# Feed-forward's first product by seven products of quarters instead of eight, and the mixing's streams in another order

## The chip, the cores and the metric

One core of a Trainium2 chip runs the whole program in one launch. The metric is device time in microseconds. Before the change three runs took 2124.88, 2127.32 and 2127.90 us (median 2127.32).

## The reference

The program is a decoder trunk of two layers over 512 tokens and 16 learned meta tokens (528 columns), model width 1024. Each layer is a half-step SwiGLU feed-forward, a token mixing of four head groups, and a second feed-forward; each has an RMS norm before and behind it. What matters here is the feed-forward:

```python
h = h + 0.5 * rms_norm(swiglu(rms_norm(h, g[0]), ffn_w_in[l, 0], ffn_w_out[l, 0]), g[1])

def swiglu(x, w_in, w_out):                 # w_in 1024 x 5120, w_out 2560 x 1024
    gate, up = jnp.split(x @ w_in, 2, axis=-1)
    return (jax.nn.silu(gate) * up) @ w_out
```

The mixing is one input product of 2476 columns, forgetting attention, a 31-tap convolution module, a gated linear recurrence, a sparse attention with a top-128 selection by an indexer, and an output product.

## The kernel before

Activations lie transposed: 128 features per tile, tokens as columns, in two halves of 264 columns (`half`, L433). The last feed-forward drops the meta tokens and has halves of 256 columns. Each fp32 operand of a large product is written as a sum of two fp32r parts, hi and lo; a product of one 128 x 128 weight tile with one tile of x is three matmuls (hi·hi, hi·lo, lo·hi; `product`, L536). A weight tile is brought by SyncE's DMA queue into one of two `raw` buffers, ScalarE copies it to hi, and VectorE (in places GpSimd) subtracts to get lo (`weight`, `wsplit`, L502 to L531). Six pairs of hi and lo buffers rotate: three of the pool `weights` and three in spare rings (`SPARE`).

The feed-forward (`ffn`, L833) goes over 20 blocks j of 128 hidden features, in chunks of 6, 6 and 8. For each block it needs a gate and an up product, each over 8 tiles of the model width, for each token half. x holds `h*g` without the norm's row factor R; `gated` (L772) multiplies both sums by R as it reads them from PSUM (VectorE), applies Silu (ScalarE), multiplies the two (GpSimd), and splits the result into G hi (ScalarE) and G lo (VectorE). In the last feed-forward the two halves are one product of 512 columns. Blocks 0 to 2 of each feed-forward (`lead`) are interleaved with the norm ahead of it. When a chunk's blocks are done, the output product adds its part to `y` (chunks 0 and 1 in `ffn`, the last one in `tail`, or in `ffn_out_tokens` for the last feed-forward).

The PSUM banks are tagged u, a and n, with 2, 5 and 1 of them (`BANKS = 251`); `pu` (L482) rotates over the seven of u and a. Temporaries of one half come from the tag `t1`, five buffers.

Two things set the order of instructions. In `ffn` it is the framework's scheduler, which takes the first instruction in program order that is ready in its own timeline. In start, mixing and the passages between feed-forwards it is `Weave` (L108 to L375): each piece of work is a stream with a rank (`RANK`), the planner has a cost for every instruction (`cost`, L199) and takes the earliest start, the lower rank among near ones; the order on each engine is then kept. `ENG` and `SUMS` say which elementwise work goes to VectorE (V), GpSimd (G) or to whichever the planner finds better (E). `ND` is the number of the 30 convolution taps per channel block that VectorE does; GpSimd and ScalarE do the others.

Of the kernel before, what the change touches and what calls it, by code (L numbers as in the profile page):

```python
# [16 lines left out]
P = 128  # L17
# [33 lines left out]
def shape_constants():  # L51
# [6 lines left out]
    c[:, C_MASK : C_MASK + 530] = np.where(j - p <= 424, 0.0, NEG)  # L58
# [49 lines left out]
class Weave:  # L108
# [13 lines left out]
    AHEAD = dict(PE=0.0, A=0.05, V=0.0, G=0.3)  # L122
# [59 lines left out]
    def ported(self, key, op, aps, reads):  # L182

        if key == "G":
            return True
        if key != "V" or any(a.space == bass.MemoryType.PSUM for a in aps) or op in ("max", "match_replace"):
            return False
        return True

    def free(self, key, ported, t):  # L190

        if not ported or key not in "VG":
            return t
        for begin, end in self.port["G" if key == "V" else "V"]:
            if begin <= t < end:
                t = end
        return t

    def cost(self, key, op, aps, args, reads, start):  # L199
# [3 lines left out]
        if key == "PE":  # L203
            if op == "transpose":
                n = args[1].shape[0]
                return self.pace(start, 0.091, n * n / 128 / 2400)
            cols, rows = args[2].free_size(), args[2].shape[0]
            if cols == 1:
                return 0.156
            if args[2].dtype == F32R:  # L210
                return self.pace(start, max(cols / 2400 + 0.0115, 0.092), cols * rows / 128 / 2400)
            return self.pace(start, max(cols * 4 / 2400 + 0.005, 0.184), cols * rows / 128 / 1200)
# [9 lines left out]
    def issue(self, key, op, call, args, kw):  # L222
# [9 lines left out]
        if key == "E":  # L232
            ways = {
                k: (self.ready(k, chip, writes), self.cost(k, op, aps, args, reads, 0.0), self.ported(k, op, aps, reads))
                for k in "VG"
            }
            if s:
                self.park(s, ("E", ways))
            key = self.either(ways)
            call, ready, _, ported = call[key], *ways[key]  # L240
        else:
            ready = self.ready(key, chip, writes)
            ported = self.ported(key, op, aps, reads)
            if s and key != "Q":
                self.park(s, (key, ready, ported))
# [3 lines left out]
        start = self.free(key, ported, max(ready, self.clock[key]))  # L249
# [5 lines left out]
        if ported:  # L255
            self.port[key] = sorted(self.port[key][-11:] + [(start, end)])
# [85 lines left out]
    def start_of(self, s):  # L342
# [7 lines left out]
        ready, ported = (what + [True])[:2]  # L350
        if kind == "E":
            kind = self.either(ready)
            ready, _, ported = ready[kind]
        return self.free(kind, ported, max(ready, self.clock[kind])), kind
# [22 lines left out]
class Trunk:  # L377
# [17 lines left out]
    KEPT = ("PE", "A", "V", "G")  # L395
    RANK = dict(ev=0, late=48.5, weights=18.0, row=179.1, lead=42.0, index=212.2, prep=19.1, scores=52.9,
                dsa=144.3, topk=187, fox=42.6, lru=14.4, lrub=76.1, first=92.5, turn0=1.5, turn1=25,
                start0=136.2, start1=79, leading=140.7, conv=0, column=99.8, link=1.1, enter=53.5,
                tail=10.4, small=2, next=79.6)
# [372 lines left out]
    def gated(self, G, pg, pu, R, c):  # L772
# [8 lines left out]
        nc.scalar.activation(G[:, 0, c], u, AF.Copy)  # L781
        nc.vector.tensor_sub(G[:, 1, c], u, G[:, 0, c].bitcast(F32))
        self.drop(*tiles)

# [48 lines left out]
    def ffn(self, l, f, w, state, final):  # L833
# [6 lines left out]
        for ch, cj in enumerate(CHUNKS):  # L840
            base = sum(CHUNKS[:ch])
            Gs = [(self.led[j], 0) for j in range(self.LEAD)] if not ch else []
            for j in range(base + len(Gs), base + cj):
                G = self.at(self.Y[j % 8], [P, 2, T], F32R, name="G")
                ws = [self.weight(wi[:, :, o + j * P : o + (j + 1) * P], KB, P) for o in (0, DFF)]
                next(params, None)
                groups = [[self.half(0, w), self.half(1, w)]] if 2 * w <= 512 else [[self.half(i, w)] for i in range(2)]
                for group in groups:
                    banks = [self.pu(), self.pu()]
                    for p, hl in zip(banks, ws):  # L850
                        self.product(p, hl, KB, x, slice(group[0].start, group[-1].stop))
                    for i, c in enumerate(group):
                        self.gated(G, *(p[:, i * w : (i + 1) * w] for p in banks), R, c)
                Gs.append((G, 0))
# [9 lines left out]
            for ob in range(KB):  # L864
                hl = self.weight(wo[:, base : base + cj, ob * P : (ob + 1) * P], cj, P)
                for half in range(2):
# [6 lines left out]
                    else:  # L873
                        nc.vector.tensor_add(yt[:, yi, c], p[:, :w], yt[:, yi, c])

# [49 lines left out]
    def ffn_out_tokens(self, l, s, ch, base, cj, wo, Gs):  # L925
# [49 lines left out]
        def leave(b):  # L975
            v = self.tiny([P, 1], "ss1", 2)
            V.tensor_reduce(v, ss[:, b * 4 : b * 4 + 4], AX.X, ALU.add)
            r = self.rsqrt_tiny(v, 1.0 / D, RMS_EPS, name=f"o{b}", factor=0.5)
# [124 lines left out]
    def mix(self, l, state, w, after):  # L1103
# [416 lines left out]
        def scores(b):  # L1520
# [3 lines left out]
            msk = self.mask[:n, 424 - QS0[b] : 424 - QS0[b] + w]  # L1524
# [15 lines left out]
        def choice(b):  # L1540
# [7 lines left out]
            if b == 1:  # L1548
                V.tensor_add(acc[:n], acc[:n], self.mask[:n, 424 - QS0[b] : 424 - QS0[b] + w])
# [55 lines left out]
        def attend(kind, b, pair):  # L1605
            if kind == "fox":
                wait("prep", "vt", f"fox{pair}")
                msk, scale = self.mask[:, 424 - QS0[b] : 424 + QN[b]], None
# [378 lines left out]
```

## Time and profile before

| | before |
|---|---|
| median of three runs | 2127.32 us |
| profiled execution | 2126.25 us |
| its span | 2124.5 us, 1.75 us less than its time |
| PE busy | 2005.0 us in 14579 matmuls |
| VectorE (DVE) busy | 1252.5 us |
| ScalarE (ACT) busy | 899.4 us |
| GpSimd (POOL) busy | 475.3 us |
| HBM read | 164.22 MB |

The four feed-forwards lie at about 36 to 340, 743 to 1060, 1112 to 1400 and 1800 to 2124 us; the mixings lie between the first and second and between the third and fourth. The line L252 is a helper that records every operation, so groups go by tiles. In the second and fourth feed-forward x is in tiles that bear the name `ycat`.

### The profile page before, as it was taken

How to read it: one execution, taken by the hardware profiler on the slowest of the kernel's cores; microseconds unless marked ns; L12 is line 12 of the kernel's file. 1: busy time of each engine (PE TensorE's matmuls, PEld its weight loads, DVE VectorE, ACT ScalarE, POOL GpSimd, SP SyncE). 2: the span in 40 equal slices, each digit the busy share in tenths (PEclk: the TensorE clock that was granted, in tenths of full speed). 3: DMA queues.
4: the chain of work that ended last, by engine and by line, in shares of the span. 5: the costliest groups of instructions: out<-in, count | busy, mean ns of one | idle time of the engine just before them, and what ended most of it. 6: DMA issues, size and time to landing. Idle time of an engine off the chain costs nothing.

```text
span 2124.5 us, 37005 instructions
## 1 busy us (share of the span) xinstructions
PE 2005.0 (94%) x14579; PEld 1880.8 (89%) x14579; DVE 1252.5 (59%) x2881; ACT 899.4 (42%) x1891; POOL 475.3 (22%) x429
## 2 busy tenths in 40 slices
PE   7999999978999899999989999999879998999998
PEld 7999999877878899999979999998768788888886
DVE  5434435889985843444384344447899958434444
ACT  5332233456765533222343322324568655332232
POOL 2101012336631110101221010123356412111121
PEclk9999999988999999999999999999889999999999
DMA  4432323211113233233223323322111132332321
GB/s 136 119 101 81 100 60 95 54 40 41 38 45 94 70 97 103 80 100 90 70 60 100 100 80 103 97 66 64 40 40 38 46 100 70 119 109 89 100 98 42
DMA packets 311078, 168.71 MB, mean 79 GB/s; under 512 B 15968, under 2 KB 302952, under 8 KB 310904
## 3 DMA queue, kind: packets, MB, share of 16 engines
q1 hardware_dynamic: 310616, 165.97, 26.9%
q8 instruction: 114, 1.87, 0.4%
q14 instruction: 60, 0.49, 0.1%
q10 hardware_dynamic: 288, 0.39, 0.1%
HBM read 164.22 MB, written 2.10 MB: 78 GB/s over the span
## 4 chain that ended last, share of the span: by engine, by line
PE 55%; DVE 21%; ACT 2%; issue 2%; SPq 1%; DMA 1%; POOL 0%; DVEq 0%; ACTq 0%; POOLq 0%
PE psa L252 39%; PE psu L252 15%; DVE msel L252 4%; DVE m L252 2%; DVE cv L252 2%; DVE hn L252 2%; PE psn L252 2%; DVE lra L252 2%; DVE acc L252 1%; DVE h L252 1%; DVE lrb L252 1%; SPq L252 1%; DVE x L252 1%; DMA wraw<-in_w_out_dram 1%; DVE rows L252 1%
## 5 line engine op out<-in xcount | busy, mean ns | idle before, releaser
L252 POOL TENSOR_TENSOR ga<-ga 128x264 f32<-128x264 f32 (+1 forms) x160 | 139.6, 874 | 1058.0 <-DVE ga L252 974.2
L252 ACT ACTIVATE whi<-wraw 128x512 fp32r<-128x512 f32 (+4 forms) x260 | 193.8, 757 | 248.7 <-PE psa L252 128.9
L252 PE MATMUL psa<-x,wh 128*128 128x264 f32 (+2 forms) x1228 | 244.8, 294 | 12.1 <-DVE x L252 4.7
L252 DVE TENSOR_TENSOR wlo<-wraw,whi 128x1024 fp32r<-128x1024 f32 (+4 forms) x179 | 179.4, 1008 | 122.1 <-ACT whi L252 120.1
L252 PE MATMUL psu<-x,whi 128*128 128x264 f32 (+1 forms) x1176 | 240.7, 300 | 6.1 <-DVE fq L252 2.7
L252 ACT ACTIVATE wh<-wraw 128x1024 fp32r<-128x1024 f32 (+3 forms) x188 | 151.3, 817 | 216.7 <-PE psa L252 117.1
L252 DVE TENSOR_TENSOR ga<-psa,R 128x264 f32<-128x264 f32 (+1 forms) x244 | 102.2, 428 | 233.5 <-PE psa L252 225.8
L252 DVE TENSOR_TENSOR wl<-wraw,wh 128x1024 fp32r<-128x1024 f32 (+3 forms) x161 | 161.4, 1011 | 127.4 <-ACT wh L252 126.3
L252 PE MATMUL psa<-x,whi 128*128 128x264 f32 (+2 forms) x1188 | 231.3, 291 | 1.0 <-DVE ga L252 1.0
L252 PEld LDWEIGHTS psa<-x,wh 128*128 128x128 f32 x1228 | 194.5, 189 | 20.4 <-DVE x L252 8.0
L252 PEld LDWEIGHTS psu<-x,whi 128*128 128x128 f32 x1176 | 192.8, 196 | 10.7 <-issue 4.2
L252 PEld LDWEIGHTS psa<-x,whi 128*128 128x128 f32 x1188 | 189.0, 191 | 2.9 <-DVE ga L252 1.1
L252 PE MATMUL psa<-x,wl 128*128 128x264 f32 (+2 forms) x614 | 178.4, 290 | 0.8 <-POOL wl L252 0.8
L252 PE MATMUL psa<-x,wlo 128*128 128x264 f32 (+2 forms) x594 | 173.1, 291 | 4.8 <-DVE wlo L252 4.8
L252 PE MATMUL psu<-x,wlo 128*128 128x264 f32 (+1 forms) x588 | 174.7, 298 | 0.0
L252 POOL TENSOR_TENSOR wlo<-wraw,whi 128x512 fp32r<-128x512 f32 (+1 forms) x81 | 116.2, 1440 | 235.9 <-ACT whi L252 207.1
L252 ACT ACTIVATE G<-ga 128x264 fp32r<-128x264 f32 (+1 forms) x160 | 67.5, 422 | 231.8 <-POOL ga L252 230.3
L252 PE MATMUL psa<-G,whi 128*128 128x264 f32 x852 | 156.4, 284 | 0.0
L252 PE MATMUL psa<-ycat,wh 128*128 128x264 f32 (+2 forms) x660 | 150.1, 318 | 3.8 <-DVE ycat L252 3.3
L252 POOL TENSOR_TENSOR cv<-cv,cm 128x528 f32<-128x528 f32 x84 | 126.4, 1505 | 91.7 <-ACT cm L252 91.6
L252 PEld LDWEIGHTS psa<-G,whi 128*128 128x128 f32 x852 | 131.8, 188 | 0.0
L252 DVE TENSOR_TENSOR G<-ga,G 128x264 fp32r<-128x264 f32 (+1 forms) x160 | 77.4, 484 | 90.3 <-ACT G L252 90.1
(306 smaller groups left out, 5030.9 us busy)
## 6 DMA issues: line engine op xcount, KB each, us to landing
wraw<-in_ffn_w_in_dram SPq DMA_DIRECT2D x160, 512.0 KB
wraw<-in_ffn_w_out_dram SPq DMA_DIRECT2D x44, 512.0 KB
wraw<-in_ffn_w_out_dram SPq DMA_DIRECT2D x48, 384.0 KB
wraw<-in_w_in_dram SPq DMA_DIRECT2D x36, 512.0 KB
wraw<-in_w_out_dram SPq DMA_DIRECT2D x180, 64.0 KB
xin<-in_x_dram SPq DMA_DIRECT2D x8, 256.0 KB
wraw<-in_w_out_dram SPq DMA_DIRECT2D x8, 256.0 KB
wraw<-in_w_in_dram SPq DMA_DIRECT2D x4, 256.0 KB
```

The lines of the kernel that those rows point to most:

```text
L252: done = call(*args, **kw)
```

## The change

Blocks 5 to 19 of each feed-forward (`PLAIN = 5`) no longer form gate and up by two products of eight tiles for each token half. The weight block [gate; up] by [first four tiles; last four tiles of the width] and the matrix [first; last four tiles] by [token half 0; 1] are taken as two 2 x 2 matrices of quarters, whose product is formed by seven products of quarters (Winograd's form of Strassen's scheme), twelve matmuls each. That needs sums and differences of the quarters of the weights (four additions for each block, `quarters`) and of x (`differences`, once in each feed-forward). Since R differs between tokens, x is rewritten with R in it: `differences` forms `h*g*R` anew, overwrites x with it, and writes three difference quarters into the rings `fq`, `fk2` and temporaries. Seven quarters (512 columns wide) are split into hi and lo; four DMAs of 256 KB replace two of 512 KB; odd blocks land in temporaries of the tag `pt`, even ones in `raw`. `seven` runs block j's first two products, then block j-1's last two, then block j's middle three. Blocks 3 and 4 keep eight products, now half 0 of both blocks first, and by halves in the last feed-forward too.

The mixing has other ranks, another order of its input product's parts, other engines for its elementwise work, and four instead of eight taps per channel block on VectorE; the planner's costs for TensorE take the weight load into account. The convolution's mask offset is written as `QS0[-1]`, which is 424 as before.

```diff
-    AHEAD = dict(PE=0.0, A=0.05, V=0.0, G=0.3)
+    AHEAD = dict(PE=0.0, A=0.19, V=0.0, G=0.3)
...
-    LB = 'a'
-    TB = 'ax'
+    LB = 'x'
+    TB = 'ux'
     LEAD = 3
+    PLAIN = 5
     WB = 3
-    ND = 8
-    ORDER = 'ccvffgqqg'
+    ND = 4
+    ORDER = 'ccvffqgqg'
...
-    SUMS = dict(tail='G', late='V', enter='E')
+    SUMS = dict(tail='V', late='V', enter='E')
...
-    ENG = dict(hadd='V', wlead='G', wt='V', wcol='G', wearly='E', wlate='G', wtail='V', wnext='E', gelu='E',
-               geluo='V', gate='V', ct='V', tapsum='E', rfox='E', rconv='E', rlru='V', rdsa='E', lrua='V',
+    ENG = dict(hadd='V', wlead='E', wt='V', wcol='G', wearly='G', wlate='G', wtail='V', wnext='E', gelu='G',
+               geluo='V', gate='G', ct='V', tapsum='E', rfox='E', rconv='V', rlru='E', rdsa='G', lrua='V',
                lrub='E', lruc='V', lrud='V', lrut='G')
...
+            plain = range(base + len(Gs), min(base + cj, self.PLAIN))
...
+            for half in range(2):
+                c = self.half(half, w)
+                for i, j in enumerate(plain):
                     banks = [self.pu(), self.pu()]
+                    for p, hl in zip(banks, ws[j]):
+                        self.product(p, hl, KB, x, c)
+                    self.gated(Gs[first + i][0], *banks, R, c)
+            Gs += self.seven(l, f, w, state, wi, range(base + len(Gs), base + cj), params)
...
+    def split_quarter(self, src):
+        hi, lo = self.quarter()
+        self.nc.scalar.activation(hi, src, AF.Copy)
+        self.nc.vector.tensor_sub(lo, src, hi.bitcast(F32))
+        return hi, lo
...
+        g1, g2, u1, u2 = q
+        W = {}
+        W["g1"] = self.split_quarter(g1)
+        W["g2"] = self.split_quarter(g2)
+        W["u2"] = self.split_quarter(u2)
+        V.tensor_add(u2, u1, u2)
+        V.tensor_sub(u1, g1, u1)
+        V.tensor_sub(g1, u2, g1)
+        W["s2"] = self.split_quarter(g1)
+        W["s3"] = self.split_quarter(u1)
+        W["s1"] = self.split_quarter(u2)
+        V.tensor_sub(g2, g2, g1)
+        W["s4"] = self.split_quarter(g2)
...
+        for k in range(4):
+            b, d, a, c = normed(k, 1), normed(k + 4, 1), normed(k, 0), normed(k + 4, 0)
+            V.tensor_sub(a, b, a)
+            V.tensor_sub(b, d, b)
+            V.tensor_sub(d, d, a)
+            V.tensor_sub(c, c, d)
+            put(d, *B["t2"][k])
+            put(b, *B["t3"][k])
+            put(c, *B["t4"][k])
+        for k in range(KB):
+            put(normed(k, 0, True), *own(k, 0))
+        for k in range(4):
+            b, a = normed(k, 1, True), normed(k, 0, True)
+            V.tensor_sub(a, b, a)
+            put(a, *B["t1"][k])
+        for k in range(4, KB):
+            put(normed(k, 1, True), *own(k, 1))
...
+        def begin(j):
...
+            mult(g.b[0], g.W["g1"], "a1", True)
+            g.s1 = keep(g.b[0], "s1", "at")
+            mult(g.b[1], g.W["g2"], "a2", True)
+            V.tensor_add(g.s1[:, :w], g.b[1][:, :w], g.s1[:, :w])
+            S.activation(g.s1[:, :w], g.s1[:, :w], AF.Silu)
...
+        def middle(g):
+            mult(g.b[0], g.W["s2"], "t2", False)
+            g.u2 = keep(g.b[0], "u2")
+            mult(g.b[2], g.W["s3"], "t3", True)
+            mult(g.b[0], g.W["s1"], "t1", False)
+            g.u4 = keep(g.b[0], "u4")
+            V.tensor_add(g.u4[:, :w], g.b[2][:, :w], g.u4[:, :w])
...
+        def end(g):
+            mult(g.b[0], g.W["s4"], "b2", False)
+            t = self.tmp(name="ga")
+            S.activation(t[:, :w], g.b[0][:, :w], AF.Silu)
+            G.tensor_mul(g.u4[:, :w], g.u4[:, :w], t[:, :w])
+            self.gate_split(g.G, g.u4, cs[1])
+            mult(g.b[2], g.W["u2"], "t4", False)
+            V.tensor_add(g.u2[:, :w], g.b[2][:, :w], g.u2[:, :w])
+            G.tensor_mul(g.u2[:, :w], g.u2[:, :w], g.s1[:, :w])
+            self.gate_split(g.G, g.u2, cs[0])
```

`normed` is one `scalar_tensor_tensor` of 264 columns on VectorE; `put` is a ScalarE copy to hi and a VectorE subtraction for lo; `keep` is a ScalarE copy out of PSUM; `gate_split` is the last two lines of `gated`; `mult` is four tiles by three matmuls into a bank, on top of what it holds where the last argument is false.

## Rows read from the trace of the kernel before

**Rows 1.** The page, parts 1 and 2: busy shares, and busy tenths of 40 slices.

```profile
PE 2005.0 (94%) x14579; PEld 1880.8 (89%) x14579; DVE 1252.5 (59%) x2881; ACT 899.4 (42%) x1891; POOL 475.3 (22%) x429
...
PE   7999999978999899999989999999879998999998
...
DVE  5434435889985843444384344447899958434444
```

**Rows 2.** Busy time by stretch, feed-forwards; stretch, length, engines (instructions), granted clock, DMA, GB/s.

```profile
850.00:903.00 53.00, 53.00 (x438) 53.00 (x437) 22.90 (x38) 15.41 (x27) 6.81 (x9) 1.00 0.27 80
1798.00:1808.00 10.00, 10.00 (x88) 10.00 (x87) 4.22 (x8) 4.46 (x8) 2.16 (x2) 1.00 0.19 55
1859.00:1912.00 53.00, 53.00 (x231) 42.98 (x230) 20.79 (x28) 18.23 (x26) 5.47 (x5) 1.00 0.37 109
```

**Rows 3.** Timeline of VectorE, first feed-forward, second chunk: start us, us, operation [idle before].

```profile
133.77 0.43 DVE L252 TENSOR_TENSOR ga<-psa,R 128x264 f32<-128x264 f32 x1 [2.49 <-PE psa L252]
135.62 0.43 DVE L252 TENSOR_TENSOR G<-ga,G 128x264 fp32r<-128x264 f32 x1 [1.42 <-ACT G L252]
...
137.69 1.23 DVE L252 TENSOR_TENSOR wl<-wraw,wh 128x1024 fp32r<-128x1024 f32 x1 [0.60 <-ACT wh L252]
...
140.59 1.42 DVE L252 TENSOR_TENSOR wl<-wraw,wh 128x1024 fp32r<-128x1024 f32 x1 [0.59 <-ACT wh L252]
```

**Rows 4.** Timeline of ScalarE, the same stretch.

```profile
135.16 0.42 ACT L252 ACTIVATE G<-ga 128x264 fp32r<-128x264 f32 x1 [3.43 <-POOL ga L252]
136.59 1.06 ACT L252 ACTIVATE wh<-wraw 128x1024 fp32r<-128x1024 f32 x1 [1.01 <-PE psa L252]
```

**Rows 5.** Timeline of GpSimd, the same stretch.

```profile
134.37 0.76 POOL L252 TENSOR_TENSOR ga<-ga 128x264 f32<-128x264 f32 x1 [40.18 <-DVE ga L252]
140.17 0.76 POOL L252 TENSOR_TENSOR ga<-ga 128x264 f32<-128x264 f32 x1 [5.04 <-DVE ga L252]
```

**Rows 6.** Timeline of VectorE ahead of the second feed-forward.

```profile
702.59 0.49 DVE L252 SCALAR_TENSOR_TENSOR ycat<-h,gT,ycat 128x264 fp32r<-128x264 f32 x1
702.99 0.43 DVE L252 TENSOR_TENSOR y<-psu,y 128x264 f32<-128x264 f32 x1
703.33 0.42 DVE L252 TENSOR_TENSOR acc<-acc,sq 128x264 f32<-128x264 f32 x1
...
712.80 0.69 DVE L252 TENSOR_TENSOR wlo<-wraw,whi 128x512 fp32r<-128x512 f32 x1
...
715.85 1.29 DVE L252 TENSOR_TENSOR wl<-wraw,wh 128x512 fp32r<-128x512 f32 x2
```

**Rows 7.** Busy time by stretch: from the norm to the fifth block's end, four feed-forwards.

```profile
36.50:81.20 44.70, 44.16 (x363) 44.16 (x364) 21.46 (x38) 17.67 (x31) 6.76 (x9) 1.00 0.32 94
743.20:780.70 37.50, 37.50 (x303) 37.50 (x302) 17.55 (x28) 13.83 (x23) 4.65 (x7) 0.97 0.35 99
1111.50:1151.10 39.60, 39.60 (x328) 39.60 (x327) 18.64 (x29) 14.15 (x24) 4.54 (x6) 1.00 0.32 94
1799.50:1833.00 33.50, 33.50 (x193) 29.34 (x192) 17.29 (x25) 13.29 (x21) 5.07 (x5) 1.00 0.50 155
```

**Rows 8.** VectorE's groups of instructions by shape, 743 to 781 us: splits of output weights.

```profile
L252 DVE TENSOR_TENSOR wl<-wraw,wh 128x768 fp32r<-128x768 f32 x3 | 2.9, 959 | 3.2 <-ACT wh L252 3.2
```

**Rows 9.** Busy time by stretch: ten microseconds behind a stall.

```profile
740.00:750.00 10.00, 10.00 (x65) 10.00 (x65) 2.89 (x10) 2.61 (x5) 0.75 (x1) 0.74 0.00 0
```

**Rows 10.** Busy time by stretch: the middles of the two mixings.

```profile
425.00:637.00 212.00, 183.16 (x1234) 160.06 (x1233) 198.03 (x573) 137.84 (x338) 103.72 (x76) 0.88 0.15 41
1470.00:1700.00 230.00, 202.41 (x1447) 179.97 (x1446) 211.91 (x633) 148.71 (x362) 108.86 (x77) 0.92 0.15 43
```

**Rows 11.** VectorE's groups of instructions by shape, middle of the first mixing.

```profile
L252 DVE SCALAR_TENSOR_TENSOR cv<-hp,taps,cv 128x528 f32<-128x528 f32 x16 | 14.2, 887 | 0.0
...
L252 DVE TENSOR_TENSOR xg<-xg 128x264 f32<-128x264 f32 x8 | 4.9, 625 | 0.0
```

**Rows 12.** GpSimd's groups of instructions by shape, middle of the first mixing.

```profile
L252 POOL TENSOR_TENSOR cv<-cv,cm 128x528 f32<-128x528 f32 x42 | 62.5, 1489 | 45.4 <-ACT cm L252 45.4
```

More of the change, by code (lines that the diff above doesn't have):

```diff
@@ L180, in pace, with hold, free @@
         return cost * (1.82 if self.slow else 1)
[L182 to L196, printed above, removed]
+    def hold(self, key, op, aps, args, reads):
+        banks = any(a.space == bass.MemoryType.PSUM for a in aps)
+        if key == "G" or key == "V" and not banks and op not in ("max", "match_replace"):
+            return self.cost(key, op, aps, args, reads, 0.0)
+        return 0.0
+    def free(self, key, hold, t):
+        if hold:
+            for begin, end in self.port["G" if key == "V" else "V"]:
+                if begin <= t < end:
+                    t = end
         return t
@@ L233, in issue @@
             ways = {
-                k: (self.ready(k, chip, writes), self.cost(k, op, aps, args, reads, 0.0), self.ported(k, op, aps, reads))
+                k: (self.ready(k, chip, writes), self.cost(k, op, aps, args, reads, 0.0),
+                    self.hold(k, op, aps, args, reads))
                 for k in "VG"
@@ L248, in issue @@
             self.clock[key] += 1.283
-        start = self.free(key, ported, max(ready, self.clock[key]))
+        start = self.free(key, hold, max(ready, self.clock[key]))
         if s:
@@ L874, in ffn, with quarter @@
                         nc.vector.tensor_add(yt[:, yi, c], p[:, :w], yt[:, yi, c])
+    def quarter(self):
+        if self.odd is None:
+            self.wturn = (self.wturn + 1) % (self.WB + len(SPARE))
+            if self.wturn < self.WB:
+                hi = self.wp.tile([P, WT], F32R, tag="whi", name="whi", bufs=self.WB)
+                lo = self.wp.tile([P, WT], F32R, tag="wlo", name="wlo", bufs=self.WB)
+            else:
+                hi, lo = (self.at(r, [P, WT], F32R, name="w" + "hl"[i])
+                          for i, r in enumerate(SPARE[self.wturn - self.WB]))
+            self.split_last[self.wturn] = lo
+            self.odd = hi, lo
+            return hi[:, : WT // 2], lo[:, : WT // 2]
+        hi, lo = self.odd
+        self.odd = None
+        return hi[:, WT // 2 :], lo[:, WT // 2 :]
@@ new lines, in seven, with mult, keep @@
+    def seven(self, l, f, w, state, wi, js, params):
+        nc = self.nc
+        V, S, G = nc.vector, nc.scalar, nc.gpsimd
+        if "parts" not in state:
+            state["parts"] = self.differences(l, 4 if f else 0, w, state)
+        self.odd = None
+        B = state["parts"]
+        cs = [self.half(i, w) for i in range(2)]
+        out = []
+        def mult(bank, quarter, part, start):
+            hi, lo = quarter
+            p = bank[:, :w]
+            for k in range(4):
+                ws = slice(k * P, (k + 1) * P)
+                xh, xl = B[part][k]
+                nc.tensor.matmul(p, hi[:, ws], xh, start=start and k == 0, stop=False, skip_group_check=not start)
+                nc.tensor.matmul(p, hi[:, ws], xl, start=False, stop=False, skip_group_check=not start)
+                nc.tensor.matmul(p, lo[:, ws], xh, start=False, stop=k == 3, skip_group_check=not start)
+        def keep(bank, name, tag="t1"):
+            t = self.tmp(name=name, tag=tag)
+            S.activation(t[:, :w], bank[:, :w], AF.Copy)
+            return t
+        def begin(j):
+            g = SimpleNamespace(W=self.quarters(wi, j), b=[self.pu() for _ in range(3)])
+            next(params, None)
+            g.G = self.at(self.Y[j % 8], [P, 2, T], F32R, name="G")
+            mult(g.b[0], g.W["g1"], "a1", True)
[3 more added lines that the diff above has]
+            S.activation(g.s1[:, :w], g.s1[:, :w], AF.Silu)
+            return g
+        def middle(g):
[15 more added lines that the diff above has]
+            self.gate_split(g.G, g.u2, cs[0])
+        last = None
+        for j in js:
+            g = begin(j)
+            if last:
+                end(last)
+            middle(g)
+            out.append((g.G, 0))
+            last = g
+        end(last)
+        return out
```

113 lines of the change are left out of this document (76 added, 37 removed).

## The prediction

> **What bounds the kernel now.** I read the page's slices first, then busy time by stretch, then the timelines of single engines. TensorE is busy for 2005 of 2124.5 us, and the slices show two kinds of stage [rows 1]. In the feed-forwards it has nines throughout while VectorE has threes and fours; in the mixings (slices 9 to 12 and 29 to 32) VectorE has eights and nines and TensorE falls to seven. By stretch, a feed-forward is TensorE and nothing else: 53.00 of 53.00 us at granted clock 1.00, 438 matmuls, so one per 0.121 us for 264 columns; 88 in 10.00 us, or 0.1136 us, for 256 columns; 231 in 53.00 us, or 0.2294 us, for 512 columns in the last feed-forward [rows 2]. VectorE is at 43% there, DMA at 0.27 to 0.37. So matmuls taken out of these stages come off the time until VectorE, whose work grows, is late.
>
> **What goes.** A block's first product is 8 x 12 = 96 matmuls, afterwards 84. In the first three feed-forwards that is 12 x 0.121 = 1.45 us for each of 15 blocks: 45 x 1.453 = 65.4 us. In the last one 48 matmuls of 512 columns (11.01 us) become 84 of 256 (9.54 us): 15 x 1.47 = 22.0 us; blocks 3 and 4 there go from 11.01 to 96 x 0.1136 = 10.91 us, together 0.2 us less. Gross: 87.6 us.
>
> **What VectorE gets.** Its prices: a 512-column subtraction lasts 0.69 us alone and two in a row 1.29, so the second starts 0.60 us after the first; of 264 columns the starts lie 0.40 us (scalar_tensor_tensor) and 0.34 us (tensor_tensor) apart [rows 6]. A block takes 7 splits and 4 additions of 512 columns, 11 x 0.60 = 6.6 us, and 5 operations of 264, 1.7 us: 8.3 us, where it was 2 x 1.23 + 6 x 0.34 = 4.5 us. TensorE needs 84 x 0.121 = 10.17 us for it (9.54 in the last feed-forward). ScalarE has 7 copies of 512 and 7 of 264; at half of 1.06 and at 0.42 us [rows 4] that is 6.7 us, not a bound. GpSimd keeps its two products for each block.
>
> A split that runs into GpSimd's product takes 1.42 instead of 1.23 us [rows 3]: GpSimd worked from 140.17 to 140.93 us [rows 5], the split began at 140.59. At 0.19 us for each of two products that is 0.4 us a block, 8.7 us in all; more than the 2 x 0.76 us that GpSimd works can't be lost, so 9.8 us is the upper bound, under 10.17 and over 9.54. [...]
>
> Whether these 8.7 us lie beside TensorE depends on the queue's order. The rows speak for it: ScalarE's split at 136.59 starts as a product frees a buffer, and VectorE's follow at 137.69 and 140.59, amid the gates of the running block [rows 3, 4]; the framework pulls weight work ahead as far as the six buffer pairs allow. After the change these hold 12 quarters, 1.7 blocks. The tightest reuse is g1 of every other block: its pair is free after block j-1's last product and it is needed three products, 4.4 us, later, for a ScalarE copy (0.53), two splits (1.2) and the hand-overs. It fits, with little room among 1.4 us of gate work. I take 0.2 us lost for each of 42 blocks and, where TensorE needs 9.54 us against 8.7 to 9.8, 0.45 us for each of 14: 15 us; bounds 0 and 60 x 1.45 = 87 us.
>
> **The rewriting of x.** `differences` has 84 VectorE operations: the first loop 16 x 0.40 + 28 x 0.34 = 15.9 us, half 0 of x 8 x 0.74 = 5.9, the quarter t1 5.9, b2 3.0; 30.7 us for each feed-forward. The first loop needs the norm's R, half 0 needs half 0 of blocks 3 and 4 to be through, t1 and b2 nearly their end. From R to that end there are 44.7, 37.5, 39.6 and 33.5 us, of which VectorE is busy for 21.5, 17.6, 18.6 and 17.3 [rows 7]. In these sums are splits which now come later or are replaced: two for block 5 (2 x 1.23) and three for output weights, 2.9 us [rows 8], in the last feed-forward 3.7. So 28.6, 25.3, 26.3 and 22.3 us are free, and first loop, half 0 and block 5's quarters want 15.9 + 5.9 + 6.6 = 28.4 us (some 0.3 less in the last). Backlog at the end of block 4: 0, 3.1, 2.1 and 5.8 us. Then come a gate (1.0), t1 (5.9), an addition (0.3), b2 (3.0) and 0.3 of hand-overs: b2 is complete 10.5 us plus backlog after that end, and TensorE, five products and nine matmuls on, wants it after 8.4. Late by 2.1 us plus backlog; the first one can start t1 early, while the last product still reads other tiles, and I take 1. Sum 1 + 5.2 + 4.2 + 7.9 = 18, say 19 us. Bounds: 0, and all of 4 x 30.7 = 123 us if nothing lies beside blocks 3 and 4. After a stall the clock falls: 65 instead of 83 matmuls in the ten microseconds at clock 0.74 [rows 9], 2.2 us; I add 4 us for two such.
>
> **Ends of chunks.** A chunk's last block has no next block to hide behind: s4 waits until `keep` has emptied its bank (a copy of 0.42 us and two hand-overs, 0.8 us), 8 times where b2 isn't late anyway, 6 us. The last gate is now of half 0, which the output product wants first. From VectorE's start at 133.77 over GpSimd's 134.37 and ScalarE's 135.16 to the end of lo at 136.05 it is 2.3 us [rows 3 to 5], with hand-overs 2.7; the output product covers 17 matmuls, 2.1 us, in a chunk of six, and all in one of eight. 6 x 0.6 = 4 us. Together 10 us, bounds 0 and 20.
>
> SyncE's queue gets 4 DMAs of 256 KB for 2 of 512 KB; the bytes stay, and with `pt` two blocks can be under way instead of one. I cost it at nothing, hidden by 10 us of products per block; without that cover a block would wait for its load.
>
> **The mixing.** In their middles VectorE is busy 198 of 212 and 212 of 230 us, GpSimd 104 and 109 [rows 10]. Off VectorE go 8 taps a layer (8 x 0.887 = 7.1 us) and the eight gelu products (8 x 0.625 = 5 us) [rows 11]; GpSimd gets the taps at 1.49 us [rows 12], and its operations hold up VectorE's. Where the new ranks put the waits can't be read from this trace. I take half of the 12 us in each layer, 12 us in all; bounds 35 gained (VectorE's 12 and some waits) and 25 lost (8 taps x 1.49 a layer in VectorE's way).
>
> **Sum.** -87.6 + 15 + 19 + 4 + 10 - 12 = -51.6. The profiled execution took 2126.25 us (its span and 1.75 us around it), 1.1 under the median; 2126.25 - 51.6 gives 2075.
>
> **Rivals.**
> A. Everything hides: the scheduler fills the gaps at the starts with output products, and the mixing gains as forecast. For it speak free stretches of VectorE and the pulling ahead [rows 3, 7]; against it that VectorE has no room at the fourth start. -87.6 + 8 - 12 gives 2035.
> B. VectorE becomes the bound of the seven-product blocks, and the kernel is slower. If its operations don't run back to back, each waiting for ScalarE's copy, a block costs 11 x 0.69 + 5 x 0.43 = 9.74 us [rows 3, 6], with full waits for GpSimd 11.2. Against 11.63 before, 45 blocks save 0.4 us and the last 15 lose 0.2: 15 us gross, against 33 us at starts and chunk ends; with the mixing 2126 - 15 + 33 - 12 = 2132. It decides from about 11.2 us a block. For it: every split has idle time before it that ScalarE ends [rows 3]; against it: the pair in 1.29 us [rows 6]. [...]
> C. The mixing loses 25 us, GpSimd's 1.49 us operations blocking VectorE: 2075 + 12 + 25 = 2112.
> D. The first loop isn't pulled ahead of the end of block 4: 16 us more in three feed-forwards: 2075 + 48 = 2123.
>
> **How the numbers follow.** Forecast 0.45 (its own range 2055 to 2095), A 0.20, B 0.11, C 0.14, D 0.10. The range is 2028 to 2125: it leaves out B and a third of A, 0.18. This kernel's runs tell a change from none at about 0.2%, 4 us: faster takes the forecast, A, C and half of D, 0.85; the same 0.04; slower 0.11.
>
> **What would show it.** There are 540 matmuls fewer in the first three feed-forwards; in the last, 816 of 512 columns (17 blocks by 48) become 1452 of 256. In the middle of a chunk TensorE stays at nines and a block takes 10.2 to 10.6 us, VectorE 85 to 95% busy; waits of TensorE for `x`, `d2`, `d3` or `wlo` ended by VectorE stand behind block 4, 1 to 8 us each. The mixings are 3 to 9 us shorter each. The prediction is wrong if a block takes over 11 us (B), if TensorE waits over 12 us behind block 4 (D), or if a mixing is longer than before (C).

## The result: 2152.6 us, 1.2% slower than before

The changed kernel takes 2152.58 us (median of 4 runs, 2149.8 to 2155.2) against 2127.14 us of the kernel before on the same chip: ratio 1.0121, 95% interval 1.0104 to 1.0139. The forecast was 2075, its range ended at 2125. The profiled execution took 2149.8 us, its span 2148.0.

The page of the changed kernel, parts 1 and 2 (busy time and instructions; busy tenths of 40 slices):

```profile
PE 1977.5 (92%) x14675; PEld 1872.9 (87%) x14675; DVE 1569.5 (73%) x3625; ACT 1116.5 (52%) x2499; POOL 540.6 (25%) x501
...
PE   8899998979989889999988999999789898999998
...
DVE  6956775899943895768488576858999638957785
```

Against [rows 1], TensorE is busy for 27.5 us less, and its count is 96 higher, which is what the forecast's 540 fewer in three feed-forwards and 636 more in the last come to. The span is 23.5 us longer all the same, so TensorE stands idle for 51 us more. VectorE has gained 317 us of work, and its threes and fours of the feed-forwards have become fives to nines.

Where the idle time lies is read by stretch (stretch, length, engines with instructions, granted clock, DMA share, GB/s): three stretches inside chunks, five behind block 4 of the second feed-forward, the ends of three feed-forwards, the middles of the mixings.

```profile
950.00:1003.00 53.00, 52.05 (x416) 50.78 (x415) 39.95 (x69) 28.93 (x64) 11.17 (x9) 1.00 0.31 90
1324.00:1377.00 53.00, 52.63 (x429) 52.24 (x428) 40.50 (x71) 29.13 (x64) 9.07 (x8) 1.00 0.30 86
2025.00:2078.00 53.00, 51.38 (x419) 49.83 (x418) 45.72 (x81) 31.08 (x69) 11.01 (x10) 1.00 0.31 90
779.00:789.00 10.00, 10.00 (x85) 10.00 (x84) 10.00 (x21) 4.82 (x10) 2.23 (x2) 1.00 0.41 119
789.00:799.00 10.00, 8.38 (x68) 8.10 (x66) 10.00 (x27) 4.08 (x10) 0.00 (x0) 1.00 0.27 80
799.00:809.00 10.00, 3.98 (x14) 2.41 (x12) 9.80 (x27) 2.97 (x8) 0.00 (x0) 0.71 0.00 0
809.00:819.00 10.00, 8.47 (x34) 7.67 (x35) 2.83 (x6) 2.35 (x5) 0.00 (x0) 0.50 0.13 39
819.00:829.00 10.00, 10.00 (x78) 9.97 (x78) 4.86 (x7) 6.33 (x14) 1.91 (x2) 0.94 0.27 81
322.00:332.00 10.00, 8.12 (x60) 7.28 (x59) 6.86 (x26) 6.49 (x13) 2.01 (x2) 1.00 0.37 108
332.00:342.00 10.00, 7.20 (x37) 6.79 (x36) 5.17 (x9) 4.84 (x10) 1.50 (x2) 0.68 0.41 121
...
1022.00:1032.00 10.00, 9.14 (x73) 8.71 (x72) 2.86 (x6) 3.26 (x9) 1.65 (x2) 1.00 0.23 67
1032.00:1042.00 10.00, 7.08 (x34) 6.57 (x33) 7.21 (x12) 5.35 (x12) 2.15 (x2) 0.66 0.55 158
1400.00:1410.00 10.00, 9.18 (x73) 8.78 (x73) 6.72 (x12) 5.18 (x11) 2.96 (x3) 1.00 0.53 158
1410.00:1420.00 10.00, 7.62 (x48) 7.21 (x47) 4.51 (x10) 4.33 (x10) 1.37 (x2) 0.83 0.52 152
...
425.00:637.00 212.00, 186.21 (x1252) 161.97 (x1251) 180.77 (x539) 146.41 (x356) 134.31 (x120) 0.89 0.16 44
1490.00:1720.00 230.00, 198.90 (x1394) 176.63 (x1394) 198.21 (x584) 155.23 (x376) 136.00 (x117) 0.91 0.14 40
```

- **Inside the chunks** TensorE is nearly full: 416 and 429 matmuls in 53 us against 438 in [rows 2], so a block of 84 takes 53 x 84/416 = 10.7 or 10.4 us. VectorE is at 75 and 76%, in the last feed-forward at 86%.
- **Behind block 4** (789 to 829 us) there are 194 matmuls where 336 would fit, 142 too few or 17 us: 9.2 us of it idle (40 less the busy 30.8). The other 8 us are matmuls that took longer, nearly all in the three stretches in which the clock is below 1.00 (34 in 8.47 busy us at 0.50, 0.25 us each); it falls to 0.50 as a mean of ten microseconds, where [rows 9] has 0.74. Until 809 us VectorE is busy nearly without a gap (10.00, 10.00 and 9.80 of 10 us).
- **At the ends** of the first three feed-forwards 71, 61 and 47 of 168 are missing, 21 us together, 12 of them idle. The rest are slower matmuls, most of it in the stretches with the clock at 0.66 to 0.83.
- **In the mixings** VectorE has 17 and 14 us less and GpSimd 31 and 27 us more than in [rows 10].

What VectorE does behind block 4 is in its timeline (start us, us, operation, idle before with its releaser). The fifth block's last gate, then the first and the last of the parts d2 to d4:

```profile
789.49 0.42 DVE L252 TENSOR_TENSOR G<-ga,G 128x264 fp32r<-128x264 f32 x1
...
794.32 0.42 DVE L252 TENSOR_TENSOR d<-xn,d 128x264 fp32r<-128x264 f32 x1
...
809.67 1.01 DVE L252 TENSOR_TENSOR d<-xn,d 128x264 fp32r<-128x264 f32 x2
```

And TensorE's timeline shows who waits for them:

```profile
792.65 0.39 PE L252 MATMUL psa<-d,whi 128*128 128x264 f32 x1 [1.62 <-ACT d L252]
...
800.76 0.99 PE L252 MATMUL psa<-d,whi 128*128 128x264 f32 x3 [1.62 <-ACT d L252]
...
805.02 1.27 PE L252 MATMUL psa<-d,whi 128*128 128x264 f32 x3 [2.18 <-ACT d L252]
...
809.00 1.27 PE L252 MATMUL psa<-d,whi 128*128 128x264 f32 x3 [1.61 <-ACT d L252]
```

So the first loop of `differences`, which of the kernel's values needs only h and R (there from 749 us on), is written last. Its tiles come from the tag `t1`, whose five buffers the gates of blocks 3 and 4 use too; these stand ahead of it in the program. That was the theory with which I began: the first loop is held by those buffers. Rivals: VectorE has no time for it, or the new mixing loses.

### The profile page after: what moved, and what is told of

Its sections match the earlier page's. It is cut to its first block, busy times and chain, and to the rows that moved or that the text cites. A ratio compares the mean times of both kernels' runs of the same rounds, so it can differ in the third digit from the quotient of the medians.

```text
span 2148.0 us, 38733 instructions
## 1 busy us (share of the span) xinstructions
PE 1977.5 (92%) x14675; PEld 1872.9 (87%) x14675; DVE 1569.5 (73%) x3625; ACT 1116.5 (52%) x2499; POOL 540.6 (25%) x501
## 4 chain that ended last, share of the span: by engine, by line
PE 59%; DVE 25%; ACT 6%; issue 3%; POOL 3%; DMA 3%; SPq 1%; ACTq 0%; POOLq 0%; DVEq 0%
PE psa L252 37%; PE psu L252 20%; DVE xn L252 4%; DVE msel L252 3%; DVE m L252 2%; PE psn L252 2%; DVE wl L252 2%; DVE acc L252 1%; ACT wh L252 1%; DVE x L252 1%; DVE lra L252 1%; DMA wraw<-in_ffn_w_out_dram 1%; DVE wlo L252 1%; DVE cv L252 1%; SPq L252 1%
## 5 line engine op out<-in xcount | busy, mean ns | idle before, releaser
L252 DVE TENSOR_TENSOR wlo<-wraw,whi 128x512 fp32r<-128x512 f32 (+3 forms) x205 | 159.5, 795 | 95.1 <-ACT whi L252 93.8
L252 DVE TENSOR_TENSOR wl<-wraw,wh 128x512 fp32r<-128x512 f32 (+2 forms) x171 | 146.7, 867 | 88.9 <-ACT wh L252 86.5
L252 ACT ACTIVATE wh<-wraw 128x512 fp32r<-128x512 f32 (+3 forms) x220 | 146.4, 677 | 123.6 <-PE psa L252 34.0
L252 PE MATMUL psa<-x,wh 128*128 128x264 f32 (+1 forms) x812 | 165.1, 298 | 15.3 <-ACT x L252 5.7
L252 PEld LDWEIGHTS psu<-x,whi 128*128 128x128 f32 x1004 | 165.4, 196 | 10.4 <-DVE gt L252 4.1
L252 PE MATMUL psa<-x,whi 128*128 128x264 f32 (+1 forms) x800 | 151.5, 286 | 3.3 <-ACT u L252 3.1
L252 PE MATMUL psa<-d,whi 128*128 128x264 f32 (+1 forms) x576 | 119.5, 300 | 15.9 <-ACT d L252 12.5
L252 PE MATMUL psa<-x,wl 128*128 128x264 f32 (+1 forms) x406 | 118.8, 293 | 0.0
L252 PE MATMUL psa<-x,wlo 128*128 128x264 f32 (+1 forms) x400 | 114.1, 286 | 0.0
L252 PEld LDWEIGHTS psu<-x,wlo 128*128 128x128 f32 x502 | 98.0, 196 | 3.6 <-POOL wlo L252 2.2
L252 PE MATMUL psa<-G,wh 128*128 128x264 f32 x524 | 98.8, 285 | 1.7 <-ACT wh L252 1.7
```

The costliest lines, as they stand in the source:

```text
L252: done = call(*args, **kw)
```

## The experiments

All ratios are to the kernel before, run on the same chip.

| run | us | ratio | 95% interval |
|---|---|---|---|
| the changed kernel | 2152.58 | 1.0121 | 1.0104 to 1.0139 |
| first loop in rings of its own | 2110.92 | 0.9921 | 0.9900 to 0.9942 |
| old mixing, seven products | 2166.09 | 1.0171 | 1.0151 to 1.0192 |
| new mixing, eight products | 2122.13 | 0.9964 | 0.9951 to 0.9977 |
| x not rewritten | 2089.15 | 0.9810 | 0.9790 to 0.9831 |
| t4 first at ends | 2112.27 | 0.9910 | 0.9894 to 0.9927 |
| first loop in four tiles | 2105.80 | 0.9883 | 0.9868 to 0.9898 |
| more cover | 2095.80 | 0.9837 | 0.9822 to 0.9851 |
| the planner's state shifted | 2109.43 | 0.9904 | 0.9889 to 0.9919 |
| t4 in a bank of its own | 2100.50 | 0.9868 | 0.9848 to 0.9889 |
| the same, four tiles | 2094.18 | 0.9834 | 0.9810 to 0.9858 |
| half 0 early | 2083.68 | 0.9789 | 0.9769 to 0.9809 |
| half 0 early, four tiles | 2079.55 | 0.9767 | 0.9740 to 0.9794 |

The next table says where the time of some of these runs lies, in us, read from the timelines of the one profiled execution of each (up to 5 us off the median above: with the rings 2115.76 against 2110.92). A feed-forward is counted from the end of ScalarE's last write of R behind its norm to the start of its last output-product matmul, the fourth to the end. The other columns are the stretches up to the first R and between the feed-forwards: the two with a mixing, and the one from the second to the third. Matmuls moved across such a mark count 0.12 us each.

| run | up to R | four feed-forwards (matmuls) | with mixing 1 | second to third | with mixing 2 |
|---|---|---|---|---|---|
| before | 36.5 | 1333.7 (9645) | 364.7 | 36.2 | 353.3 |
| the changed kernel | 36.4 | 1352.8 (9700) | 360.3 | 40.5 | 358.1 |
| first loop in rings | 38.4 | 1300.4 (9720) | 364.3 | 43.6 | 367.3 |
| old mixing, seven products | 37.7 | 1354.1 (9709) | 365.3 | 37.2 | 369.7 |
| new mixing, eight products | 36.1 | 1330.2 (9617) | 368.5 | 35.8 | 349.6 |
| x not rewritten | 36.6 | 1291.4 (9698) | 358.1 | 39.1 | 363.4 |
| t4 first at ends | 37.5 | 1299.8 (9710) | 362.8 | 43.9 | 368.8 |
| more cover | 37.4 | 1291.4 (9739) | 357.1 | 44.0 | 362.7 |
| half 0 early | 37.7 | 1275.1 (9713) | 360.9 | 43.5 | 362.8 |

**1. The first loop in rings of its own.**

```
-  b, d, a, c = normed(k, 1), normed(k + 4, 1), normed(k, 0), normed(k + 4, 0)
+  four = self.at(("fk", "qd", "gl", "cv0")[k], [P, 4, H2], name="xf")
+  b, d, a, c = (normed(i, half, into=four[:, n]) for n, (i, half) in
+                enumerate(((k, 1), (k + 4, 1), (k, 0), (k + 4, 0))))
```

> The first loop of differences takes its 16 tiles from four rings that are free there (fk, qd, gl, cv0) and not from the five t1 buffers that it shares with the gates of blocks 3 and 4; nothing else differs from the changed kernel. Theory 1 (the first loop is held by those buffers: its fourth tile waits for a gate of block 4, so 48 VectorE instructions run behind block 4 and TensorE waits for them): the parts d2 to d4 are written while blocks 3 and 4 are multiplied, the waits of TensorE on ScalarE's d (3.7 to 7 us in a feed-forward) go, and with them most of the clock's fall; the four first chunks, 388.8 us together in the changed kernel, come to 345 to 360 us, the whole to 2110 to 2122 us. Rival 1 (VectorE has no time for the rewriting anywhere in these stretches): the work only changes places, the first chunks stay within 10 us of 388.8, the whole at 2142 to 2155 us.

0.9921: from 1.2% slower to 0.8% faster, 0.0200 or 42.6 us. VectorE's timeline shows the loop beginning right behind R (743 us here) and its last part written 25 us after it, where it was 61 in the changed kernel:

```profile
743.76 2.10 DVE L252 SCALAR_TENSOR_TENSOR xf<-h,gT,R 128x264 f32<-128x264 f32 x5
...
754.58 0.43 DVE L252 TENSOR_TENSOR d<-xf,d 128x264 fp32r<-128x264 f32 x1
...
768.25 0.42 DVE L252 TENSOR_TENSOR d<-xf,d 128x264 fp32r<-128x264 f32 x1
```

Behind block 4 TensorE is nearly full and the clock holds (by stretch, as above):

```profile
783.00:793.00 10.00, 10.00 (x84) 10.00 (x83) 10.00 (x24) 4.18 (x10) 1.05 (x1) 1.00 0.50 146
793.00:803.00 10.00, 9.15 (x75) 8.94 (x74) 6.53 (x12) 4.57 (x9) 1.52 (x2) 1.00 0.16 49
803.00:813.00 10.00, 10.00 (x84) 10.00 (x84) 3.30 (x4) 5.36 (x13) 0.00 (x0) 1.00 0.60 176
```

VectorE does the same work (3625 instructions, 1565.5 us busy against 1569.5), so the rival that it has no time for it falls. Of TensorE's waits (what for, us in total, times, longest), these are the changed kernel's

```profile
PE psa L252 <- ACT d L252: 19.4, 12, 2.2
PE psa L252 <- ACT u L252: 11.9, 17, 1.6
...
PE psa L252 <- ACT G L252: 5.4, 2, 2.7
...
PE psu L252 <- ACT G L252: 4.1, 2, 2.3
PE psu L252 <- ACT d L252: 3.7, 2, 2.1
```

(23.1 us for `d` in both rows) and these what is left of them with the rings: the one for `d` is gone.

```profile
PE psa L252 <- ACT u L252: 6.1, 11, 1.8
...
PE psa L252 <- ACT G L252: 4.5, 2, 2.7
PE psu L252 <- ACT G L252: 4.3, 2, 2.5
```

By place all four feed-forwards are shorter, by 11.8, 16.1, 13.5 and 11.0 us, 52 in all; the stretches between them are 16 us longer, and why isn't shown.

**2. The first loop in four tiles.** One ring, allocated again in each of the four turns: `self.at("fk", [P, 4, H2], name="xf")`.

> The first loop of differences in four tiles of one ring, used again in each of its four turns: one tile fewer than the five of the t1 buffers, but none shared with a gate. Theory (what held it was the order in which the t1 buffers are handed out, behind the gates of blocks 3 and 4): it still runs beside those blocks, the whole within 6 us of the kernel with 16 tiles, 2105 to 2117 us. Rival (the number of tiles was what lacked): 2130 us or more.

0.9883, no slower than with 16. Four tiles are fewer than t1's five; what held the loop was the sharing with the gates, not the number.

**3. x not rewritten.** Both loops of `differences` are replaced by a constant in d2 to d4.

```
-  for k in range(4): ...          (both loops)
+  for t in (d2, d3, *d4):
+      nc.gpsimd.memset(t.bitcast(F32), 0.5)
```

> The changed kernel without the rewriting of x: the parts d2 to d4 are filled with a constant by GpSimd and x stays as it is without its norm, so the products are of other numbers; the number of TensorE's instructions and the gates are as in the changed kernel. It gives the whole price of the rewriting with what follows from it. Theory 1 (the rewriting behind block 4 and the clock after it are what the first chunks lose): the four first chunks come from 388.8 us to 335 to 345, and the whole to 2095 to 2108 us. Rival 1 (the seven-blocks' VectorE and gates are the loss, the rewriting is a small part of it): 2135 us or more.

0.9810: 0.0311 or 66 us under the changed kernel, 24 us under the run with the rings. The time fell below my band. So 43 of 66 us came from where the first loop stood, and 24 us are what the rewriting costs the whole program when it starts in time. By place only 9 of the 25 us between these two profiled runs lie in the feed-forwards, and 15 in the stretches between them, where nothing is rewritten; why isn't shown.

**4. The mixing by itself, both ways.** One run gives the changed kernel the old planner, ranks, engines and tap count; the other gives the kernel before the new ones.

```
-  ND = 4      ORDER = 'ccvffqgqg'   wearly='G' gelu='G' gate='G' ...
+  ND = 8      ORDER = 'ccvffgqqg'   wearly='E' gelu='E' gate='V' ...
```

> The changed kernel with the planner, the ranks, the engines of the mixing and its number of VectorE taps as they were before; the feed-forwards keep seven products. Theory 1 (the new order of the mixing loses 13.9 us by itself, 1.6 in the first and 12.4 in the second): about 2138 us, the mixings back at 329.6 and 316.6 us within 3 us. Rival (the mixing is late because of the state in which the feed-forward leaves the queues and buffers): the mixings stay at about 331 and 329 us, the whole at 2150 to 2156 us.

> The kernel before with the new planner, ranks, engines and four VectorE taps, and eight products in the feed-forwards. Theory 1 (the new order loses by itself): about 2127 + 14 = 2141 us. The prediction's term (the mixing gains 12 us): 2115 us. Rival (it loses only with seven products ahead of it): 2124 to 2130 us.

My theory, that the new order loses, was wrong both times. With eight products it gains 0.36% (7.7 us, 5 to 10); with seven, taking it away costs 0.50% (10.6 us). I had read its loss from the time between two norms of the trace (316.6 us before, 328.9 after), but the new order also moves work across those marks. The feed-forward with seven products is what loses: 1.0171 over 1, or 1.0121 over 0.9964, 1.6 to 1.7% either way. By place not all of that is in the feed-forwards themselves: with seven products the stretch with mixing 2 is longer in either order, 369.7 us against 353.3 in the old (3 of these 16 us are 25 matmuls moved into it) and 358.1 against 349.6 in the new.

**5. More cover for the copy of a bank.** In the steady blocks TensorE now and then waits for ScalarE's copy of a bank (`u2` or `u4`, both `u` in the views) before it may write that bank again.

```
   mult(g.b[0], g.W["s2"], "t2", False)
   g.u2 = keep(g.b[0], "u2")
+  if last:
+      end0(last)      # u2 by t4 of the block before: from ahead of s2 to here
   mult(g.b[2], g.W["s3"], "t3", True)
```

> As the run with t4 first at the ends, and in the other blocks u2 by t4 of the block before is put behind s2 by t2, so that 24 instead of 12 products cover ScalarE's copy of the bank (u2) before the bank is written again; s2 by t2 itself has 12 products less ahead of it. Theory (the steady loss of the seven-blocks, 0.4 to 0.7 us in each where the forecast had 0.2 to 0.45, is the wait for this copy): 5 to 12 us less than that run. Rival (the copies are late because VectorE and ScalarE are busy with weights, and the wait moves to s1's sum or the gate): within 3 us of it.

0.9837 against 0.9910 of the run it was built on: 15.5 us, more than expected. The waits for `u` in the `psa` banks, 7.2 us in that run and 6.1 with the rings alone, fall to 3.9 (TensorE's waits, kernel with more cover), while those for the gate stay:

```profile
PE psa L252 <- ACT u L252: 3.9, 8, 1.1
PE psu L252 <- ACT G L252: 3.8, 2, 2.0
PE psa L252 <- ACT G L252: 3.6, 2, 2.7
```

These waits explain 3 us of it. The steady blocks give some 5: in 53 us inside the second feed-forward's last chunk TensorE runs 415 matmuls with the rings and 418 with more cover, 0.08 us for each of 60 blocks.

```profile
930.00:983.00 53.00, 52.06 (x415) 50.77 (x415) 40.74 (x70) 29.39 (x65) 11.29 (x9) 1.00 0.30 86
...
915.00:968.00 53.00, 51.95 (x418) 51.05 (x417) 39.55 (x69) 28.93 (x64) 11.07 (x8) 1.00 0.31 90
```

By place, of the 20 us between the two profiled runs 7 lie in the first feed-forward, 1 in the other three together (5 if the 29 matmuls moved into the feed-forwards are allowed for) and the remaining 8 to 12 between the feed-forwards, where the edit does nothing. So the theory accounts for a part, and for most of the gain the cause is open.

**6. The end of a chunk, in three tries.** First only the order in the program was turned around (u2 by t4 ahead of s4 by b2).

> The kernel with the first loop in the rings, and in the last block of each chunk u2 by t4 and the gate of half 0 ahead of s4 by b2 and the gate of half 1, since the next product reads half 0 first; nothing else. Theory (the end of a chunk costs what this gate makes TensorE wait, 2.7 us at three tails and 1.7 in the last feed-forward, with the clock's fall behind it, some 50 of 84 instructions in 10 us): the wait on ScalarE's G at the tails goes, 4 to 6 us at each of four, 2090 to 2098 us against 2110.9. Rival (the tail is held by its weights, which come late from the queue in any case): 2106 to 2112 us, with the wait on a weight in the gate's place.

0.9910, as without it. TensorE's timeline says why: s4 by b2 (`x`) still runs ahead of u2 by t4 (`d`), since t4's bank must wait for the sum that reads s3's product, and the framework issued what was ready. The wait on the gate is unchanged.

```profile
1009.86 0.40 PE L252 MATMUL psu<-x,whi 128*128 128x264 f32 x2
...
1010.59 0.40 PE L252 MATMUL psa<-d,whi 128*128 128x264 f32 x2
...
1014.93 0.39 PE L252 MATMUL psa<-G,whi 128*128 128x264 f32 x1 [2.71 <-ACT G L252]
```

Second, t4 gets a bank of its own (`mult(g.b[1], g.W["u2"], "t4", True)` and one more sum) in the run with more cover.

> As the run with more cover; in the last block of a chunk u2 by t4 goes to a bank of its own (one more sum on VectorE), so that it needn't wait for the sum that reads s3's bank and can really be multiplied, and half 0 gated, ahead of s4 by b2. (In the run with t4 first at the ends the order of the instructions had not changed: t4 still stood last.) Theory (the end of chunk 2 costs the wait of 2.7 us on the last gate at the tails, 1.8 to 2.5 in the first and last feed-forward, and the clock's fall after it): 4 to 6 us at each of four ends, 2072 to 2082 us against 2095.8, with TensorE's wait on G under 1 us at the tails. Rival (the tail waits for its weights in the gate's place): the wait on whi or wlo takes over, 2090 to 2098 us.

0.9868, not faster than 0.9837: a miss again. Now the order is right, but in ScalarE's timeline a tail weight's copy, itself behind a DMA, stands before both gates:

```profile
994.57 1.15 ACT L252 ACTIVATE wh<-wraw 128x512 fp32r<-128x512 f32 x2 [0.91 <-DMA wraw<-in_ffn_w_out_dram]
995.63 0.37 ACT L252 ACTIVATE ga<-psu 128x264 f32<-128x264 f32 x1
995.90 0.41 ACT L252 ACTIVATE G<-u 128x264 fp32r<-128x264 f32 x1
997.20 0.42 ACT L252 ACTIVATE G<-u 128x264 fp32r<-128x264 f32 x1 [0.89 <-POOL u L252]
```

TensorE's wait for the gate stayed, at 3 us. The same with four tiles:

> The run with t4 in a bank of its own, with the first loop in the four tiles of one ring in place of 16. Both theories of the first loop have it within 5 us of that run; it is the candidate for the best version, since the run with four tiles came out 5 us under the one with 16.

0.9834, 7 us under its twin. Third, half 0 is finished 24 products before the block's end:

```
   mult(g.b[2], g.W["s3"], "t3", True)
+  if final:           # a chunk's last block
+      mult(g.b[1], g.W["u2"], "t4", True)
+      ...             # two sums, the gate and the split of half 0
   mult(g.b[0], g.W["s1"], "t1", False)
```

> As the run with more cover; in the last block of a chunk u2 by t4 (in a bank of its own) and the gate of half 0 come ahead of s1 by t1 and s4 by b2, so 24 products stand behind the gate of half 0 and the next 24 read half 0 alone. (With t4 only just ahead of s4 the wait of 3 us stayed: from the last sum to the finished gate it took 4.3 us, as the copy of a tail weight stood before it on ScalarE.) Theory (chunk ends cost this wait and the clock behind it): the waits on G at the tails fall under 1 us, 2078 to 2088 us against 2095.8 to 2100.5 of the two runs it builds on. Rival (the tail's weights, on DMA until some 20 us later, hold it): 2093 to 2100 us, with waits on weights.

> The same with the first loop in the four tiles of one ring. In two pairs of runs four tiles were 5 to 6 us faster than 16; if that is the order on VectorE, where the first loop then stands spread among the gates of the first blocks, and no chance, it is so again: 3 to 8 us under the run with 16 tiles. If it was chance: within 3 us.

0.9789 and 0.9767; the second is 2.3% under the kernel before and the fastest of all here. The wait at the second feed-forward's end falls from 2.7 to 1.4 us, not under 1 (all of TensorE's waits for ScalarE's G from 7.4 to 1.9 us), and with it the clock holds. Ends by stretch, first of the run with more cover, then of the one with half 0 early:

```profile
990.00:1000.00 10.00, 7.52 (x57) 7.10 (x57) 5.72 (x10) 4.84 (x11) 3.08 (x3) 1.00 0.18 55
1000.00:1010.00 10.00, 8.82 (x59) 8.58 (x60) 6.01 (x11) 4.21 (x8) 0.32 (x1) 0.83 0.71 209
```

```profile
990.00:1000.00 10.00, 8.73 (x70) 8.32 (x68) 7.41 (x13) 5.00 (x11) 2.44 (x3) 1.00 0.56 159
1000.00:1010.00 10.00, 9.75 (x78) 9.55 (x79) 5.56 (x11) 5.43 (x12) 0.00 (x0) 1.00 0.58 160
```

116 matmuls become 148: 3.8 us at one of four ends, where the whole gained 10.2 (0.0048). By place the four feed-forwards gain 4.8, 4.4, 2.9 and 4.2 us (2.5 of the last are 21 matmuls moved out of it), so most of this gain lies where the edit was aimed. Four tiles in place of 16 were 8, 7 and 5 us faster in three pairs, of which the last two have intervals that overlap.

**7. The planner's state.** The planner's clocks were set, at each session, to where they stood in the run with the new mixing alone.

```
+  d = (5.48, 419.46, 1192.48, 1646.08)[self.nth] - w.clock["PE"]
+  w.clock = {k: t + d for k, t in w.clock.items()}      # and the marks
```

> The kernel with the first loop in the rings, and the planner's clocks and times are shifted at each session so that they stand where they stood in the run with the new mixing alone (its model of TensorE's clock goes by windows counted from its zero, so a feed-forward of another modelled length gives another order of the streams); nothing else. Theory (mixing 2 with its tail and lead, 417.6 us here and 399.5 there, is longer because the planner found another order): 398 to 406 us there, the whole 2095 to 2103 us. Rival (it is longer because of the real state of queues and buffers behind the seven-blocks): 412 us or more there, the whole 2106 to 2114 us.

0.9904, within the interval of 0.9921; the second mixing with its tail and lead (from the third feed-forward's last gate to the last one's norm) took 412.0 us, at the rival's bound. It was 399.5 and 400.4 us in the two kernels with eight products and 406 to 420 in all twelve with seven. Why is open: neither the new order (399.5) nor this shift accounts for it.

## Why the prediction was wrong

**The step that failed** is the backlog at the end of block 4, and in it the sentence "The first loop needs the norm's R". It also needs buffers. I counted VectorE's free time between R and the end of block 4 and let 15.9 us of first loop flow into it; but its tiles come behind the gates' in the turn of `t1`, so that time lay open and the loop came behind block 4. This is rival D (0.10). Its price, 16 us in each of three feed-forwards, 48 in all, lies near the 42.6 measured, but in part by luck: all four feed-forwards lost, 52 us together, slower matmuls among them (8 of the 17 us behind block 4 of the second), and the stretches between took 16 us the other way. D's own sign, over 12 us of waiting behind block 4, wouldn't have shown it: TensorE was idle there for 9.2 us.

**The rewriting that is left.** 19 + 4 = 23 us forecast, 23.6 measured (0.9921 less 0.9810) once the loop starts in time. That the two agree is luck too: the forecast puts all of it behind block 4, and by place some 9 us are in the feed-forwards.

**Gross and steady loss.** The count of matmuls is exact. I had 10.17 + 0.2 = 10.4 us a block; the stretches give 10.4 and 10.7. In the last feed-forward, 9.99 forecast, 419 in 53 us gives 10.6. So 0 to 0.3 us a block more than forecast, and 0.6 in that stretch of the last feed-forward. Most of this 0.6 is a wrong price: the 88 in 10.00 us of [rows 2] that I took for 256 columns include four matmuls of 128 columns and some cut by the stretch's edges. In the timeline of the kernel before, 48 matmuls of 256 columns take from 1799.26 to 1804.95 us, 0.1185 us each where I had 0.1136, and 229 of 512 columns start within the 53 us, 0.2314 us each. A block of 84 then takes 9.95 us and not 9.54, and the last feed-forward gains some 17 us gross and not 22. VectorE was cheaper than forecast, 75 to 86% busy where I had 85 to 95. Rival B doesn't hold: it needs 11.2 us and a full VectorE.

**Ends of chunks.** Forecast 10 us, at most 20; three ends alone miss 21 us of matmuls. I had priced the wait (2.7 us on the gate, which I had only partly counted, since 17 or all matmuls were to cover it) and not the slower clock behind it.

**These two together.** Without the rewriting my sum would have been 2075 - 23 = 2052 us; the run measured 0.9810 x 2127.3 = 2086.9, 35 us more. By place, the four feed-forwards of that run are 42 us shorter than before, 5 of them because 43 matmuls moved out, where 87.6 less 25 for steady loss and ends makes 63. So they are some 26 us short, 5 of them the price of 256 columns and some 20 steady loss and ends. The rest lies outside the feed-forwards, where I had 12 us of gain and, the moved matmuls allowed for, 1 us was lost: the stretch with mixing 2 alone is 10 us longer. That a stretch without a seven-product block gets longer behind such blocks had no term in my sum, and its cause is open (experiment 7). Of the two edits aimed at steady loss and ends, half 0 early gave 10.2 us back, mostly where it was aimed; more cover gave 15.5, only a part of it there.

**The mixing.** Forecast -12, measured -7.7 with eight products and -10.6 with seven: right in sign and nearly in size. Rival C has not come; my sign of it ("a mixing is longer than before") would have misled, as experiment 4 shows.

**The outcome lies above D's 2123**, because D took the forecast's other terms along: 2075 + 42.6 + the 35 us above gives 2152.6. (These parts are differences between runs, so that they add up proves nothing.) The version with the first loop in four tiles, more cover and half 0 early comes to 0.9767, or 2078 us; that this is near 2075 is no support for the forecast, which priced the changed kernel without those edits.

## What to carry to other kernels

When work is to be pulled ahead into free time, list what it needs as three things: data, an engine, and a buffer. Look who takes buffers of the same tag earlier in the program. A reorder in the source must be checked in the timeline: one here changed nothing. Price a stall of TensorE at nearly twice its length where the clock falls behind it (here 17 us for 9.2 idle and 21 for 12). And before a gain gets the name of the edit's reason, read by stretch where it lies: of two edits here that made the program faster, one did so mostly where it was aimed, and of the other's gain a good half lies in stretches that it doesn't touch or is unexplained.

## What was not expected of the hardware

- After waits of 1.6 to 2.2 us, four within 18 us, TensorE's granted clock was 0.71, 0.50 and 0.94 in three successive stretches of ten microseconds: half of full speed for the whole of the middle one (0.50 in each two microseconds from 805 to 819), with 34 matmuls in 8.47 us of busy time. In the kernel before it was 0.50 from 735 to 745 us. Of the 17 us lost in 40, 9.2 were idle and nearly all the rest lies in these three stretches.
- GpSimd's 264-column product took 756 ns in the steady blocks of the kernel before (VectorE 43% busy) and 1371 and 1092 ns in those of the changed one (75%). Its groups by shape, 950 to 1003 us, changed kernel (count, busy us, mean ns, idle before), and ahead of them the one of 850 to 903 us in the kernel before:

```profile
L252 POOL TENSOR_TENSOR ga<-ga 128x264 f32<-128x264 f32 x9 | 6.8, 756 | 45.8 <-DVE ga L252 45.8
...
L252 POOL TENSOR_TENSOR u<-u,ga 128x264 f32<-128x264 f32 x5 | 6.9, 1371 | 70.0 <-DVE wq L252 43.0 <-ACT ga L252 20.3 <-DVE u L252 6.7
L252 POOL TENSOR_TENSOR u<-u,s 128x264 f32<-128x264 f32 x4 | 4.4, 1092 | 3.6 <-DVE u L252 3.6
```

In the timelines of that stretch three 512-column subtractions of VectorE that began during one of these products took 1.24 to 1.25 us (at 971.90, 983.13 and 994.55 us), where one alone takes 0.69 [rows 6]. Of the products, two that began during a subtraction took 1.64 and 2.24 us (968.47 and 990.52), and the one that ran while VectorE stood idle took 0.75 (981.32). I had charged the overlap to VectorE alone, at 0.19 us for each product; GpSimd's product lengthens too, and it is part of the gate that TensorE waits for at a chunk's end.
